# State space stage: real and imaginary parts of a group on the two halves of the partitions

## The chip, the cores and the metric

The kernel runs on one core of a Trainium2 chip. The metric is device time in microseconds for one call; the time before is the median of three runs. The core's engines are TensorE (PE, with its weight loads PEld), VectorE (DVE), ScalarE (ACT), GpSimd (POOL) and SyncE (SP), which issues transfers. Each takes its own instructions in a fixed order.

## The reference

The program is one step of a two-layer encoder: 2048 prompt positions and 8 samples of 16 positions, width 1024. Layer 0 is a diagonal complex state space mixer (S5), layer 1 a gated delta-rule mixer; each is normalised and modulated, and a last norm follows. The part that is changed is the core of layer 0. It has 64 groups of 16 channels, and each group has 64 complex states:

```python
def step(carry, uc):
    hr, hi = carry
    br = jnp.einsum('gpc,btgc->btgp', bbr, uc)
    bi = jnp.einsum('gpc,btgc->btgp', bbi, uc)
    pr, pi, sr, si = lax.associative_scan(_cplx_combine, (a_r, a_i, br, bi), axis=1)
    xr = pr * hr[:, None] - pi * hi[:, None] + sr
    xi = pr * hi[:, None] + pi * hr[:, None] + si
    y = jnp.einsum('gcp,btgp->btgc', c_re, xr) - jnp.einsum('gcp,btgp->btgc', c_im, xi)
    return (xr[:, -1], xi[:, -1]), y
```

In words: an input product gives a complex drive per state, a first-order complex recurrence runs over time, and an output product takes the real part of C times the state. The output then goes through a gelu, a gated linear unit and an output projection.

## The kernel before, in words

Time is cut into chunks of 8 positions, so a group's 16 channels times 8 positions fill 128 rows, and a chunk is one column: 256 columns of the prompt and 16 of the samples, 272 in all (`NCH`, with `NPC` = 256). Inside a chunk the recurrence is a small triangular matrix (`toe`) on the input; between chunks only the state matters.

The stage takes the 64 groups in 16 batches (`b`) of four: two pairs (`pl`), and in each pair two groups (`g2`, or `i`), one on partitions 0 to 63 and one on 64 to 127. So a state tile is `[128, 2 (pair), 2 (r: real, imaginary), 272]`: the partition halves are the two groups of a pair, and real and imaginary parts lie side by side in each partition.

`s5_setup(b)` makes a batch's matrices: VectorE builds the input matrix `abt` (L672 to L674), TensorE transposes it (L679) and ScalarE copies it out as `ab`; VectorE builds the output matrix `ca` (L685 to L687), which `split_w` splits into a high part (ScalarE's cast, L130) and a low part (VectorE's subtraction, L131) so that a product of three reduced-precision terms (high by high, high by low, low by high) keeps the precision; a product `pk` gives the triangular matrix, which is written to DRAM as `kp` (GpSimd clears it at L699, VectorE corrects it at L701, ScalarE issues the write at L702) and read back as `toe`.

`s5_main(b)` does the work. TensorE makes the drive `pb` for each pair (L732), ScalarE copies the sample columns out as `bs` (L735), VectorE turns by the rotation table into `f` (L737) and sums to `z` (L739, L740), scans two segments with a carry `cy` between them (L746 to L753), turns back into `t` (L760), and builds the states before each chunk, `x`, by a difference and a sum (L762, L763). The samples' columns of `x` come from the given states (L722) and L738. `x` is split into `xsh` and `xsl` like a weight (L130, L131). The output is one product `toe` by `u` (L772) and, per group, six products over its 64 partitions (L777): two parts by three terms. ScalarE applies the gelu (L781) and the result goes to DRAM.

TensorE has a second supply of work in the stage: the z projection, 64 blocks (`z_block`) of 24 products over 128 rows, called `pdz` in the trace, which depend on nothing in the stage. The last six blocks are held back behind the stage's last outputs. The weights of the next stage (`wgr`, split into `wg`) load into memory that the stage gives up at its end.

The order of each engine's instructions is fixed when the program is built: a scheduler plays the program through with its own durations and sets each engine's order by that. The buffers bound how far batches overlap: most tiles of `s5_main` have two buffers (pool `b2`), `kp` and the work tiles `tt` and `abt` one, `pb` one in PSUM, the outputs two.

Of the kernel before, what the change touches and what calls it, by code (L numbers as in the profile page):

```python
# [10 lines left out]
F32 = mybir.dt.float32  # L11
# [3 lines left out]
ALU = mybir.AluOpType  # L15
# [3 lines left out]
P = 128  # L19
# [3 lines left out]
NCH = 272  # L23
NPC = 256
# [29 lines left out]
def kernel(ctx: ExitStack, tc: tile.TileContext, I, O, upto="Z"):  # L54
# [19 lines left out]
    T, V, S, G, SY = (Engine(e) for e in (nc.tensor, nc.vector, nc.scalar, nc.gpsimd, nc.sync))  # L74
# [54 lines left out]
    def split_w(dst_hi, dst_lo, raw, lo_eng=None):  # L129
        S.copy(dst_hi, raw)  # L130
        (lo_eng or V).tensor_sub(dst_lo, raw, dst_hi.bitcast(F32))  # L131
# [102 lines left out]
    with ExitStack() as pa:  # L234
# [333 lines left out]
        for j in range(8):  # L568
            hh, hl = hcur
            T.ordered = j == 1  # L570
            for cb in range(8):
# [14 lines left out]
                if j > 0:  # L586
                    ps = psd4.tile([P, NCH], F32, tag="d", name=f"pd{j}_{cb}")
                    i_ = mm3(ps, ks(wu_hi[cb]), ks(wu_lo[cb]), hh, hl)
# [43 lines left out]
    with ExitStack() as pb:  # L632
        ps5 = pb.enter_context(ExitStack())
        b2 = ps5.enter_context(tc.tile_pool(reuse_waits="tile", name="b2", bufs=2))
        b1 = ps5.enter_context(tc.tile_pool(reuse_waits="tile", name="b1", bufs=1))
# [25 lines left out]
        def s5_setup(b):  # L661
# [8 lines left out]
            tt = b1.tile([P, 2, 2, 9, 16], F32, tag="tt", name=f"abtt{b}")  # L670
# [13 lines left out]
            for l in range(2):  # L684
                V.tensor_mul(ca[:, l], bc(bc(ccv[:, 0, l], 1, 9), 1, 2), bc(pw[:, l, 1:3], 3, 16))  # L685
                V.tensor_mul(t2[:, l], bc(bc(ccv[:, 1, l], 1, 9), 1, 2), bc(pw[:, l, 0:2], 3, 16))
            V.tensor_sub(ca, ca, t2)  # L687
            cs_ = [b2.tile([P, 2, 2, P], F32R, tag="ca" + i, name=f"ca{i}{b}") for i in "hl"]
            split_w(*(t.rearrange("p l r (n c) -> p (l r) n c", c=16) for t in cs_),
                    ca[:, :, :, 1:9].rearrange("p l r n c -> p (l r) n c"))  # L690
# [25 lines left out]
        def s5_main(b, u, tw, ca, ab, toe):  # L716
# [3 lines left out]
            xh = x[:, :, :, NPC:NCH].rearrange("p l r (q h) -> p l r q h", h=2)  # L720
            G.memset(x[:, :, :, 0:1], 0.0)
            S.copy(xh[:, :, :, :, 0], stN[:, prs])  # L722

# [4 lines left out]
            for pl in range(2):  # L728
# [9 lines left out]
                V.tensor_add(xh[:, pl, :, :, 1], ax[:, 2 * b + pl], bsv[:, :, :, 0])  # L738
            V.tensor_add(z[:, :, 0], f[:, 0, :, 0], f[:, 1, :, 1])  # L739
# [22 lines left out]
            V.tensor_sub(x[:, :, 0, 1:NPC], t[:, 0, :, 0, 0:m], t[:, 1, :, 1, 0:m])  # L762
            V.tensor_add(x[:, :, 1, 1:NPC], t[:, 0, :, 1, 0:m], t[:, 1, :, 0, 0:m])  # L763
# [4 lines left out]
            for pl in range(2):  # L768
# [4 lines left out]
                for r in range(2):  # L773
                    for wi, xi in ((0, 0), (0, 1), (1, 0)):
                        for i in range(2):
                            ln = slice(64 * i, 64 * i + 64)
                            i_ = T.matmul(pys[i], lhsT=ca[wi][ln, pl, r], rhs=xs[xi][ln, pl, r],  # L777
                                          start=False, stop=(r == 1 and wi == 1), tile_position=(64 * i, 0))
# [41 lines left out]
    with ExitStack() as px:  # L820
# [104 lines left out]
        for j in range(8):  # L925
# [78 lines left out]
            r = acc  # L1004
# [1094 lines left out]
```

## Time and profile before

| What | us |
|---|---|
| Median of 3 runs | 2154.48 |
| Lowest and highest | 2152.29, 2161.67 |
| Span of the profiled execution (it has no time listed beside this) | 2147.2 |
| TensorE busy | 2083.9 (97%) |
| VectorE busy | 1558.8 (73%) |
| ScalarE busy | 980.2 (46%) |
| GpSimd busy | 473.6 (22%) |

The page's shares are means over a long program; TensorE's 97% is modelled from pipelined matmuls, whose rows overlap: where the trace gives 0.29 us for one, the next starts 0.125 us later. The state space stage takes about 316 of the 2147 us. A row of the timeline gives the start, the duration of the group, engine, line, operation, written and read tile with partitions by elements, and a count; a form 64*128 is a matmul over 64 rows, and 128*128 one over 128.

### The profile page before, as it was taken

The page shows a single profiled execution, that of the slowest core. Times are in us where ns is not written, and L with a number is a line of the kernel's source. Part 1 is how long each engine was busy: PE and PEld are TensorE (multiplying, and loading weights), DVE is VectorE, ACT ScalarE, POOL GpSimd, SP SyncE. Part 2 cuts the span into 40 slices and gives each one's busy share as a digit, 9 for nine tenths or more (in the row PEclk, how much of TensorE's full clock was granted, in tenths as well). Part 3 has the DMA queues.
Part 4 walks back from the last instruction along what each step waited for, and adds up shares of the span by engine and source line. Part 5 has one row for each costly group of instructions (what it writes and reads, how often), then busy time and mean ns, then how long its engine had stood idle before and what let it go on. Part 6 is the DMA issues. An engine that isn't in the chain of part 4 may idle for free.

```text
span 2147.2 us, 42222 instructions
## 1 busy us (share of the span) xinstructions
PE 2083.9 (97%) x15729; PEld 1851.3 (86%) x15729; DVE 1558.8 (73%) x4017; ACT 980.2 (46%) x2298; POOL 473.6 (22%) x720
## 2 busy tenths in 40 slices
PE   6899999999799999999999999999999899999998
PEld 4888988888599999999888879889987688888887
DVE  6999498999756554446665669688556788888875
ACT  3543433333255544446665422341224556666663
POOL 1267310000112322222100000100011344444430
PEclk9999999999899999999999999999999999999999
DMA  9897744444386533336465313663456844444432
GB/s 278 273 299 234 239 150 149 141 157 148 97 242 220 190 113 110 108 100 218 138 202 171 92 50 86 162 146 103 135 169 217 269 143 126 134 142 147 147 113 70
DMA packets 398666, 344.99 MB, mean 161 GB/s; under 512 B 88410, under 2 KB 359274, under 8 KB 398460
## 3 DMA queue, kind: packets, MB, share of 16 engines
q1 hardware_dynamic: 261388, 234.95, 36.9%
q10 hardware_dynamic: 134256, 99.69, 14.4%
q0 software_dynamic: 2816, 7.65, 1.0%
q8 instruction: 124, 2.03, 0.4%
q14 instruction: 82, 0.67, 0.1%
HBM read 221.40 MB, written 120.80 MB: 159 GB/s over the span
## 4 chain that ended last, share of the span: by engine, by line
PE 86%; DVE 6%; DMA 4%; ACT 2%; issue 1%; SPq 1%; POOL 0%; ACTq 0%; DVEq 0%
PE epo L69 6%; PE pc L150 5%; PE pc L152 5%; PE pc L151 5%; PE pz L152 3%; PE po L150 3%; PE pz L151 3%; PE pdz L151 3%; PE pz L150 3%; PE po L152 3%; PE po L151 3%; PE pdz L150 3%; PE pdz L152 3%; PE pg L152 3%; PE pg L150 3%; PE pg L151 3%
## 5 line engine op out<-in xcount | busy, mean ns | idle before, releaser
L150 PE MATMUL pc<-h1h,wdh 128*128 128x512 f32 (+1 forms) x600 | 216.5, 361 | 0.0
L152 PE MATMUL pc<-h1h,wdl 128*128 128x384 f32 (+1 forms) x600 | 214.9, 358 | 0.0
L151 PE MATMUL pc<-h1l,wdh 128*128 128x384 f32 (+1 forms) x600 | 214.8, 358 | 0.1
L1414 DVE SCALAR_TENSOR_TENSOR ac<-pb,convw,ac 128x384 f32<-128x384 f32 (+3 forms) x288 | 163.6, 591 | 3.3
L150 PE MATMUL pdz<-hhz,wzh 128*128 128x272 f32 x512 | 152.3, 298 | 1.8 <-ACT evz L627 1.8
L151 PE MATMUL pdz<-hlz,wzh 128*128 128x272 f32 x512 | 153.0, 299 | 0.0
L152 PE MATMUL pdz<-hhz,wzl 128*128 128x272 f32 x512 | 151.6, 296 | 0.0
L150 PE MATMUL po<-gh,woh 128*128 128x272 f32 x512 | 148.6, 292 | 2.2 <-ACT gh L942 2.2
L151 PE MATMUL po<-gl,woh 128*128 128x272 f32 x512 | 148.4, 291 | 0.8 <-DVE gl L942 0.8
L152 PE MATMUL po<-gh,wol 128*128 128x272 f32 x512 | 148.7, 292 | 0.0
L151 PE MATMUL pg<-yl,wgh 128*128 128x272 f32 x512 | 148.4, 290 | 0.0
L150 PE MATMUL pg<-yh,wgh 128*128 128x272 f32 x512 | 147.5, 288 | 0.5 <-ACT evz L627 0.5
L152 PE MATMUL pg<-yh,wgl 128*128 128x272 f32 x512 | 147.5, 288 | 0.0
L150 PEld LDWEIGHTS pc<-h1h,wdh 128*128 128x128 f32 x600 | 112.6, 188 | 12.3 <-issue 1.7
L151 PEld LDWEIGHTS pc<-h1l,wdh 128*128 128x128 f32 x600 | 112.7, 188 | 10.4 <-issue 0.8
L152 PEld LDWEIGHTS pc<-h1h,wdl 128*128 128x128 f32 x600 | 112.6, 188 | 10.2 <-issue 0.8
L150 PE MATMUL pd<-hh,wuh 128*128 128x272 f32 x384 | 112.5, 294 | 0.0
L69 PE MATMUL epo<-w2h,ohi 128*128 128x512 f32 x272 | 111.7, 410 | 0.0
L152 PE MATMUL pd<-hh,wul 128*128 128x272 f32 x384 | 110.9, 289 | 0.0
L151 PE MATMUL pd<-hl,wuh 128*128 128x272 f32 x384 | 110.6, 288 | 0.0
L69 PE MATMUL epo<-w2l,ohi 128*128 128x512 f32 x272 | 107.5, 395 | 1.6 <-DMA w2l<-w2l_d 1.5
L939 POOL TENSOR_TENSOR zt<-zt,sz 128x272 f32<-128x272 f32 x64 | 63.4, 996 | 203.5 <-ACT sz L938 194.3
(613 smaller groups left out, 6373.7 us busy)
## 6 DMA issues: line engine op xcount, KB each, us to landing
wa<-in_w_ada SPq DMA_DIRECT2D x32, 512.0 KB
wdr<-in_w_in SPq DMA_DIRECT2D x24, 512.0 KB
h_d<-x ACTq DMA_DIRECT2D x8, 1088.0 KB
u_d<-ev ACTq DMA_DIRECT2D x64, 136.0 KB
hz<-h_d SPq DMA_DIRECT2D x16, 544.0 KB
u<-u_d SPq DMA_DIRECT2D x16, 544.0 KB
z_d<-evz ACTq DMA_DIRECT2D x64, 136.0 KB
y_d<-y ACTq DMA_DIRECT2D x32, 272.0 KB
```

Of the source, the lines that this page charges most:

```text
L69: i_ = f(*a, **kw)
L150: T.matmul(ps, lhsT=w_hi[k], rhs=x_hi[k], start=(k == 0), stop=False)
L151: T.matmul(ps, lhsT=w_hi[k], rhs=x_lo[k], start=False, stop=False)
L152: i_ = T.matmul(ps, lhsT=w_lo[k], rhs=x_hi[k], start=False, stop=(k == n - 1))
L939: G.tensor_mul(zt, zt, sz)
L1414: V.scalar_tensor_tensor(o, src(j), convw[:, b, j:j + 1], o, op0=ALU.mult, op1=ALU.add)
```

## The change

The output product is to contract over the real and the imaginary part of one group at once. For that `x` gets another layout: real parts on partitions 0 to 63 and imaginary parts on 64 to 127, with the group of the pair beside them in the free dimension, `[128 (r, state), 2 (pair), 2 (g2), 272]`. `ca` gets the same one. What stands before (`pb`, `f`, `z`, the scans, `t`) keeps the old layout.

So there are new steps. In `s5_setup` ScalarE copies four quarters of `ca` into a new tile `cax` (it shares the single buffer `tt`), and the split reads that. In `s5_main` the sample columns are built in a tile of their own, `xh`, and ScalarE copies four quarters of it into `x`. The difference and the sum that build `x` become four operations over 64 partitions each: two stay on VectorE (they move data to the other half), two go to GpSimd (they keep it in its half). Each group's output is then three products over 128 rows in place of six over 64.

```diff
             V.tensor_sub(ca, ca, t2)
+            cx = b1.tile([P, 2, 2, 9, 16], F32, tag="tt", name=f"cax{b}")
+            for r in range(2):
+                for g2 in range(2):
+                    S.copy(cx[64 * r:64 * r + 64, :, g2, 1:9], ca[64 * g2:64 * g2 + 64, :, r, 1:9])
             cs_ = [b2.tile([P, 2, 2, P], F32R, tag="ca" + i, name=f"ca{i}{b}") for i in "hl"]
-            split_w(*(t.rearrange("p l r (n c) -> p (l r) n c", c=16) for t in cs_),
-                    ca[:, :, :, 1:9].rearrange("p l r n c -> p (l r) n c"))
+            split_w(*(t.rearrange("p l g (n c) -> p (l g) n c", c=16) for t in cs_),
+                    cx[:, :, :, 1:9].rearrange("p l g n c -> p (l g) n c"))
...
-            xh = x[:, :, :, NPC:NCH].rearrange("p l r (q h) -> p l r q h", h=2)
+            xh = b2.tile([P, 2, 2, 8, 2], F32, tag="xh", name=f"xh{b}")
             G.memset(x[:, :, :, 0:1], 0.0)
             S.copy(xh[:, :, :, :, 0], stN[:, prs])
+            halves = (slice(0, 64), slice(64, 128))
...
+            for r, rl in enumerate(halves):
+                for g2, gl in enumerate(halves):
+                    S.copy(x[rl, :, g2, NPC:NCH], xh[gl, :, r].rearrange("p l q h -> p l (q h)"))
...
-            V.tensor_sub(x[:, :, 0, 1:NPC], t[:, 0, :, 0, 0:m], t[:, 1, :, 1, 0:m])
-            V.tensor_add(x[:, :, 1, 1:NPC], t[:, 0, :, 1, 0:m], t[:, 1, :, 0, 0:m])
+            for r, op in enumerate((ALU.subtract, ALU.add)):
+                for g2, gl in enumerate(halves):
+                    (G if g2 == r else V).tensor_tensor(x[halves[r], :, g2, 1:NPC], t[gl, 0, :, r, 0:m],
+                                                        t[gl, 1, :, 1 - r, 0:m], op=op)
...
-                for r in range(2):
-                    for wi, xi in ((0, 0), (0, 1), (1, 0)):
-                        for i in range(2):
-                            ln = slice(64 * i, 64 * i + 64)
-                            i_ = T.matmul(pys[i], lhsT=ca[wi][ln, pl, r], rhs=xs[xi][ln, pl, r],
-                                          start=False, stop=(r == 1 and wi == 1), tile_position=(64 * i, 0))
+                for wi, xi in ((0, 0), (0, 1), (1, 0)):
+                    for i in range(2):
+                        i_ = T.matmul(pys[i], lhsT=ca[wi][:, pl, i], rhs=xs[xi][:, pl, i], start=False, stop=(wi == 1))
```

Line numbers after the change are higher by up to 10 (the output products stand at L785, `t` at L768, `x` at L772).

The scheduler plays the new program through and moves instructions all over the stage. On TensorE, at the output products of batch 0's first pair (`py_0` and `py_1` are the two groups' outputs, `pdz` the z projection):

```order
+L785 MATMUL py_0_4277<-xsl_4273,cah_4147 128x272
+L785 MATMUL py_1_4278<-xsl_4273,cah_4147 128x272
+L785 MATMUL py_0_4277<-xsh_4272,cal_4148 128x272
+L785 MATMUL py_1_4278<-xsh_4272,cal_4148 128x272
 L150 MATMUL pdz_1_6555<-hhz_1_6355,wzh_4040 128x272
 L151 MATMUL pdz_1_6555<-hlz_1_6356,wzh_4040 128x272
 L152 MATMUL pdz_1_6555<-hhz_1_6355,wzl_4041 128x272
-L777 MATMUL py_0_4260<-xsl_4256,cah_4142 128x272
-L777 MATMUL py_1_4261<-xsl_4256,cah_4142 128x272
-L777 MATMUL py_0_4260<-xsh_4255,cal_4143 128x272
-L777 MATMUL py_1_4261<-xsh_4255,cal_4143 128x272
```

Before, six more rows of the other part follow; now four rows finish what ten did.

On TensorE again, where the z projections of the stage end. Before, they last until just ahead of the outputs of batch 14 (`py_0_6136`) and the drive of batch 15 (`pb_0_6180`):

```order
L150 MATMUL pdz_1_7971<-hhz_1_7771,wzh_4040 128x272
L151 MATMUL pdz_1_7971<-hlz_1_7772,wzh_4040 128x272
L152 MATMUL pdz_1_7971<-hhz_1_7771,wzl_4041 128x272
L772 MATMUL py_0_6136<-u_5907,toe_5948 128x272
L772 MATMUL py_1_6137<-u_5907,toe_5948 128x272
L732 MATMUL pb_0_6180<-u_6041,ab_6054 64x272 x4
L732 MATMUL pb_1_6189<-u_6041,ab_6054 64x272 x4
```

Now they end inside the outputs of batch 11 (`py_0_5751` to `py_3_5766`), ahead of the drive of batch 12 (`pb_1_5844`):

```order
L785 MATMUL py_1_5752<-xsh_5746,cal_5543 128x272
L151 MATMUL pdz_1_7971<-hlz_1_7772,wzh_4040 128x272
L152 MATMUL pdz_1_7971<-hhz_1_7771,wzl_4041 128x272
L737 MATMUL pb_1_5844<-u_5644,ab_5657 64x272 x4
L699 MATMUL pk_5814<-ca_5798,sp_5782 32x128 x4
L782 MATMUL py_2_5765<-u_5510,toe_5556 128x272
L785 MATMUL py_2_5765<-xsh_5746,cah_5542 128x272
```

The same z products thus lie in twelve batches instead of fourteen.

On GpSimd, about batches 2 to 4. Before there were only memsets (`kp` of batches 5 and 6, the first column of `x` of batches 3 to 5):

```order
L721 MEMSET xs_4614 128x4
L699 MEMSET kp_4737 64x112
L721 MEMSET xs_4748 128x4
L699 MEMSET kp_4871 64x112
L721 MEMSET xs_4882 128x4
```

Now the two operations on `x` of batches 2 and 3 (`xs_4490`, `xs_4624`) stand between them:

```order
L703 MEMSET kp_4613 64x112
L772 TENSOR_TENSOR xs_4490<-t_4532 64x2x255 x2
L725 MEMSET xs_4758 128x4
L703 MEMSET kp_4747 64x112
L772 TENSOR_TENSOR xs_4624<-t_4666 64x2x255 x2
```

So `x` of a batch now queues behind the clearing of `kp` for a batch two further on.

## The prediction

> **What bounds the kernel now.** I read the busy times by stretch first, then the waits, then the ends of the chain, and last the timelines of TensorE and VectorE inside the stage. By stretch (busy time of each engine, granted clock, DMA share):
>
> ```profile
> core 0: us, PE busy (x) PEld busy (x) DVE busy (x) ACT busy (x) POOL busy (x), PEclk, DMA share, GB/s
> 270.00:310.00 40.00, 40.00 (x322) 35.08 (x320) 39.07 (x81) 13.39 (x31) 5.69 (x13) 1.00 0.42 130
> 310.00:550.00 240.00, 240.00 (x1845) 199.77 (x1843) 219.12 (x467) 83.48 (x209) 3.54 (x24) 1.00 0.49 150
> 550.00:586.00 36.00, 25.31 (x148) 17.58 (x146) 30.63 (x54) 7.81 (x21) 8.43 (x9) 0.78 0.23 80
> ```
>
> The state space stage lasts from 270 to 586 us. In its middle TensorE never rests and VectorE works 219.12 of 240 us: two engines near their limit, the second with 9% to spare. At the end TensorE is short of work, and VectorE sets the pace. The waits inside the stage (in total, times, longest) and the end of the chain:
>
> ```profile
> DVE f L737 <- ACT bs L735: 20.4, 10, 4.5
> ACT bs L735 <- PE pb L732: 29.0, 23, 4.0
> ...
> 584.83 0.60 DVE xs L763
> 585.66 0.34 SPq L796
> 586.05 4.61 DMA wgr<-in_w_glu
> ```
>
> VectorE's spare time is 20.4 us of waiting at L737 for the input product pb, which comes late from TensorE's queue behind z projections. The chain shows what the stage's end decides: only when the last x is built do the next stage's weights start to load. So what the stage loses reaches the end of the kernel.
>
> Where x is complete gives the pace, batch 0 and batch 11:
>
> ```profile
> 301.84 0.68 DVE L763 TENSOR_TENSOR xs<-t 128x510 f32<-128x510 f32 x1
> 512.97 0.68 DVE L763 TENSOR_TENSOR xs<-t 128x510 f32<-128x510 f32 x1
> ```
>
> 211.1 us for 11 batches, 19.2 each; then 73.1 us to 586.
>
> **The output products.** TensorE's timeline around one group of them:
>
> ```profile
> 308.78 0.29 PE L151 MATMUL pdz<-hlz,wzh 128*128 128x272 f32 x1
> 308.91 0.28 PE L152 MATMUL pdz<-hhz,wzl 128*128 128x272 f32 x1
> 309.12 0.39 PE L777 MATMUL py<-xsl,cah 64*128 64x272 f32 x2
> 309.35 0.29 PE L777 MATMUL py<-xsh,cal 64*128 64x272 f32 x2
> 309.47 0.29 PE L777 MATMUL py<-xsh,cah 64*128 64x272 f32 x2
> 309.60 0.29 PE L777 MATMUL py<-xsl,cah 64*128 64x272 f32 x2
> 309.73 0.29 PE L777 MATMUL py<-xsh,cal 64*128 64x272 f32 x2
> 309.94 0.39 PE L150 MATMUL pdz<-hhz,wzh 128*128 128x272 f32 x1
> 310.18 0.29 PE L151 MATMUL pdz<-hlz,wzh 128*128 128x272 f32 x1
> ```
>
> A full product over 128 rows takes a slot of 0.125 us (308.78 to 308.91). A pair of the old products, one on each half of the rows, also takes one slot: the two run side by side. So 24 half products make 12 slots a batch, and the 12 full products of the change make 12 slots: halving their number saves nothing in itself. What goes is entering and leaving the half-row form: from 308.91 to 310.18 stand seven slots (0.88 us) in 1.27 us, 0.39 us too much per group. The order has 48 groups, three a batch: 1.17 us a batch, 18.7 us in all, are saved on TensorE.
>
> **What x costs now.** VectorE keeps two operations a batch, over 64 partitions instead of 128 and as long per partition (510 elements). I take the old 0.60 us from start to start for each: partitions don't set the time, elements do. Nothing is saved there. GpSimd gets two more, which VectorE did before. An operation of that length on GpSimd, and what it does to VectorE, stands in two places: a row of groups, and batches 14 and 15, the same VectorE work without and with GpSimd at work.
>
> ```profile
> L1219 POOL TENSOR_TENSOR olo<-ob,ohi 128x512 fp32r<-128x512 f32 x30 | 37.8, 1282 | 130.6 <-ACT ohi L69 130.6
> ```
>
> ```profile
> 559.47 0.69 DVE L739 TENSOR_TENSOR z<-f 128x512 f32<-128x512 f32 x1
> 560.08 0.68 DVE L740 TENSOR_TENSOR z<-f 128x512 f32<-128x512 f32 x1
> 560.68 1.36 DVE L746 TENSOR_TENSOR_SCAN z<-rN,z 128x128 f32<-128x128 f32 x4
> ...
> 562.55 0.86 DVE L746 TENSOR_TENSOR_SCAN z<-rN,cy,z 128x128 f32<-128x128 f32 x2
> ...
> 572.39 1.78 DVE L739 TENSOR_TENSOR z<-f 128x512 f32<-128x512 f32 x1
> 574.10 1.10 DVE L740 TENSOR_TENSOR z<-f 128x512 f32<-128x512 f32 x1
> 575.12 3.04 DVE L746 TENSOR_TENSOR_SCAN z<-rN,z 128x128 f32<-128x128 f32 x4
> ...
> 580.10 1.61 DVE L746 TENSOR_TENSOR_SCAN z<-rN,cy,z 128x128 f32<-128x128 f32 x4
> ```
>
> ```profile
> 571.41 2.20 POOL L797 TENSOR_TENSOR ax<-ax,bs 128x512 f32<-128x512 f32 x1 [18.89 <-DVE xs L738]
> 573.70 0.96 POOL L648 TENSOR_TENSOR stN<-ax,a 128x256 f32<-128x256 f32 x1
> ...
> 578.76 1.29 POOL L799 TENSOR_TENSOR stN<-stN,bs 128x512 f32<-128x512 f32 x1
> ```
>
> L739 takes 1.78 instead of 0.69 us while GpSimd's 512-element operation runs: 1.09 us lost. Over the whole stretch (559.47 to 562.55 against 572.39 to 580.10) VectorE loses 4.63 us to eight GpSimd operations of 2560 elements together, which is 0.92 us for 510. The upper bound is GpSimd's own 1.28 us. I take 1.1, the row of the nearest shape: 2.2 us a batch, 35 us over 16 batches (bounds 29 and 41). It falls on nearly every operation that follows in VectorE's order, since those too combine two tiles in SBUF; the lower end of all, nothing, is the first rival.
>
> The Trainium skill, SBUF — State Buffer, section Who interferes with whom, has a rule for this: a VectorE operation with two inputs in SBUF and a GpSimd operation that reads SBUF share a read interface, and the later waits for the whole of the other. By that rule each would cost the full 1.28 us and my sum would be some 6 us higher; the trace agrees in kind and lies a little below.
>
> **The other edits.** ScalarE gets eight copies a batch. Rows to price them:
>
> ```profile
> L130 ACT CAST xsh<-xs 128x1088 fp32r<-128x1088 f32 x16 | 17.6, 1100 | 16.9 <-DVE xs L763 14.7 <-DMA z_d<-evz 2.2
> L130 ACT CAST cah<-ca 128x512 fp32r<-128x512 f32 x16 | 9.9, 620 | 39.2 <-PE py L777 32.9 <-DMA k_d<-kp 3.6 <-DVE ca L687 2.8
> ```
>
> That is 0.83 ns an element, so 0.41 us for each of four copies of 256 elements into cax, and some 0.22 for each of four of 32 into x: 2.5 us a batch beside the 83.48 of 240 us that ScalarE works now, so it fits. The cax copies lie a batch ahead of their use, with VectorE work between ca and the low part; the copies into x wait for nothing late. If that cover failed, each batch would pay the 2.2 us of the copies and the cast. No DMA is added: SP has 579 rows before and now.
>
> What grows is the way from t to the low part of x: formerly two operations and the cast, 1.2 + 1.1 us; now two of GpSimd and two of VectorE in turns and the cast, some 3.8 + 1.1 us. Behind it on VectorE stands xsl, and behind that the next batch's f. In most batches three or four operations stand ahead of xsl and fill the cast's time as before; in batch 10 and three of the last four there is only the sum into xh (old L738), and about 1.2 us each is bare.
>
> **The sum, stretch by stretch.** *Batch 0:* VectorE is full (39.07 of 40), so its 2.2 us count: +2 (0 to 5).
>
> *Batches 1 to 11:* the new order puts 1132 z products there instead of 965 (counted from the last output product of batch 0 to that of batch 11). TensorE: 167 more slots are +20.9 us, 33 groups less are -12.9, so 219.1 instead of 211.1 us. VectorE: 219.12/240 of 19.2 is 17.5 us a batch, plus 2.2 is 19.7, or 216.7 us. Two engines that need 219 and 217 us and wait for each other at pb and at x don't both stay full. Before, the spare of VectorE (1.7 us a batch) let TensorE run without a gap; I allow 1 us a batch of new waiting: 230, +19. Bounds: +8 (no new waiting) and +28 (VectorE's 1.7 us of waiting stays, and GpSimd costs 1.28).
>
> *Batches 12 to 15:* no z product is left there in the new order (but for the last 20, inside batch 15's outputs), so VectorE decides. Its operations in the new order, each priced from start to start as in batch 14, are 47 us for f to xsl of four batches and 13 for the setup that is left; the old GpSimd work at the end takes 4.6, the new 8.8, the bare waits 3.6: 77 against 73.1, so +5 with the last batch's longer way (0 to 9). TensorE's clock falls there (0.78 already in the last 36 us), but each pb has ten or more us of VectorE work ahead of its use, or x and xsl; I add nothing.
>
> Together +26. The profiled execution would span 2173 instead of 2147.2 us; the median of the runs shown is 7.3 us above that span, so I add to the median: 2154.5 + 26 = 2180. The forecast's own range, by the three bounds, is 2162 to 2197.
>
> **The rivals.** *GpSimd doesn't hold VectorE up here, and the saved switches carry.* It speaks for it that VectorE waits 20.4 us anyway and that GpSimd is nearly idle (3.54 of 240); against it L739's 1.78 us. Then the middle goes by TensorE, +8, and the last batches by VectorE without the 8.8 us and without the earlier waits, 60 + 4.6 = 65 us against 73, -8: no change, 2154. It decides if an operation of GpSimd costs VectorE under about 0.3 us. Should also the 8 us of z products hide in ScalarE's and VectorE's waits of the middle, it is 2146.
>
> *GpSimd's queue delays x.* Memsets of kp now stand ahead of x in the same queue, and each waits for the DMA that reads the batch before:
>
> ```profile
> POOL kp L699 <- DMA k_d<-kp: 172.4, 15, 16.3
> ```
>
> So far nobody waited behind it. If it makes x 1.5 us late in each of 16 batches, 24 us come on top: 2204. Against it, in the order kp's correction on VectorE stands ten us or more before that x in all but one batch.
>
> **How the numbers follow.** Forecast 0.62, first rival 0.21 (a third of it below no change), second rival 0.13, something unseen 0.04. The time is the forecast's, 2180. The range goes from 2157, inside the first rival, to 2205, the second's time. A measurement here tells 0.5% from no change, that is 2143.7 to 2165.3: faster 0.07 (the third of the first rival), same 0.18 (its rest and the forecast's low edge), slower 0.75.
>
> **What would show it.** Right: no 64*128 form is left, and output products cost 0.125 us each with no gap around them; L672 to L690 and the scans on VectorE keep their length where GpSimd rests, while those behind t grow by about 1 us twice a batch; GpSimd's x operations last 1.3 to 2.2 us; TensorE idles over the last four batches; the first wgr load starts near 612 instead of 586. Wrong: VectorE's busy time in the stage grows by under 10 us (first rival), or GpSimd waits for k_d while VectorE waits for xsh (second); a pace of batches 1 to 11 under 19.9 or over 21.8 us would break the middle term.

## The result and the profile after

The changed kernel takes 2179.23 us (median of 4 runs, 2177.92 to 2180.46), the kernel before 2153.39 us beside it: ratio 1.0114, 95% interval 1.0095 to 1.0132. It is 25 us slower. The forecast was 2180.

Its profiled execution spans 2177.8 us. For one reading the reader has to know that the profiled execution of before (2147.2 us) was among the quickest of its kernel, whose medians in five comparisons were 2153 to 2158 us. Differences between profiles therefore come out some 5 us larger than the ratios. Below, prices come from ratios, and places from profiles.

Busy time by engine, first the whole program before, then after:

```profile
PE 2083.9 (97%) x15729; PEld 1851.3 (86%) x15729; DVE 1558.8 (73%) x4017; ACT 980.2 (46%) x2298; POOL 473.6 (22%) x720
```

```profile
PE 2076.7 (95%) x15537; PEld 1852.6 (85%) x15537; DVE 1582.1 (73%) x4017; ACT 1018.3 (47%) x2426; POOL 535.0 (25%) x752
```

VectorE executes as many instructions as before, two of the old ones a batch being half as wide now, and is busy 23.3 us longer. GpSimd has 32 instructions and 61 us more, ScalarE 128 and 38 us more. TensorE is 7.2 us less busy, and that is all the saved output products show.

The stretches of the stage after the change, without its first 40 us (busy time of PE, PEld, DVE, ACT and POOL, granted clock, DMA share and GB/s); the last of them belonged to the next stage before:

```profile
310.00:550.00 240.00, 230.36 (x1705) 202.91 (x1703) 220.57 (x422) 108.24 (x292) 37.41 (x43) 1.00 0.47 144
550.00:586.00 36.00, 20.97 (x82) 12.97 (x83) 34.73 (x70) 10.66 (x31) 6.88 (x8) 0.58 0.26 79
586.00:618.00 32.00, 12.17 (x53) 7.17 (x51) 27.43 (x45) 8.52 (x25) 13.64 (x12) 0.73 0.21 69
```

TensorE now rests 9.6 us in the middle, where it had none to spare. At the end it works about half of the time, and VectorE nearly all of it. The end of the stage, in the chain of waits:

```profile
610.87 2.37 DVE t L768 x2
...
613.26 0.69 DVE xs L772
613.96 1.65 DVE xs L772
615.64 1.15 DVE fsp L801
...
617.37 3.91 DMA wgr<-in_w_glu
```

The next stage's first weights start to load at 617.4 instead of 586.05 us, and from there to the end both kernels need the same (1560.4 and 1561.2 us). So the loss lies ahead of that point. Some of it was there when the stage began: VectorE's first operation on `abt` (L672) starts at 270.68 us in this profile and at 267.10 in the one of before, 3.6 us late.

The same, cut where VectorE starts the low part of x (`xsl`, L131) in batch 0, in batch 11 and in batch 15; before and after:

```profile
304.24:515.10 210.86, 210.86 (x1623) 175.34 (x1622) 194.47 (x412) 74.05 (x182) 3.25 (x22) 1.00 0.49 152
515.10:586.65 71.55, 60.21 (x418) 46.84 (x417) 60.90 (x119) 20.71 (x53) 8.83 (x12) 0.88 0.34 108
```

```profile
307.27:539.90 232.63, 225.71 (x1680) 200.58 (x1680) 215.04 (x410) 102.49 (x275) 37.41 (x43) 1.00 0.47 146
539.90:617.90 78.00, 40.44 (x179) 25.13 (x178) 70.32 (x130) 25.01 (x73) 20.63 (x21) 0.69 0.25 79
```

These 15 batches took 282.4 us and take 310.6. VectorE's busy time in them (third of the busy columns) was 255.4 and is 285.4; what is left is its waiting, 27.0 and 25.3. From x to x the stage is longer by VectorE's work, and its old waiting time has not shrunk to pay for that. Of the 30 us more work some 23 are new by the page; the rest is mostly preparation of matrices that lay ahead of batch 0's x before.

### The profile page after: what moved, and what is told of

The parts are those of the page before. It is cut to its first block, busy times and chain, and to the rows that moved or that the text cites. A ratio compares the mean times of both kernels' runs of the same rounds, so it can differ in the third digit from the quotient of the medians.

```text
span 2177.8 us, 41988 instructions
## 1 busy us (share of the span) xinstructions
PE 2076.7 (95%) x15537; PEld 1852.6 (85%) x15537; DVE 1582.1 (73%) x4017; ACT 1018.3 (47%) x2426; POOL 535.0 (25%) x752
## 4 chain that ended last, share of the span: by engine, by line
PE 71%; DVE 15%; DMA 7%; ACT 3%; issue 3%; POOL 1%; SPq 1%; ACTq 0%; DVEq 0%; POOLq 0%
PE epo L69 7%; PE pc L150 5%; PE pc L152 5%; PE pc L151 5%; PE pz L152 3%; PE pz L151 3%; PE pz L150 3%; PE po L150 3%; PE po L152 3%; PE po L151 3%; PE pg L152 2%; PE pg L150 2%; PE pg L151 2%; PE epx L69 2%; PE pdz L150 2%
## 5 line engine op out<-in xcount | busy, mean ns | idle before, releaser
L150 PE MATMUL pc<-h1h,wdh 128*128 128x512 f32 (+1 forms) x600 | 216.6, 361 | 0.2 <-ACT pb L1410 0.2
```

Source lines behind the costliest of these rows:

```text
L150: T.matmul(ps, lhsT=w_hi[k], rhs=x_hi[k], start=(k == 0), stop=False)
```

## The experiments

Each variant changes some lines, and with them the scheduler's order of the whole stage; its price is that of the edit and of the order that comes with it. The table sums up; "x to x" is the stretch from batch 0's `xsl` to batch 15's, with VectorE's busy time and its waiting in it. These three columns come from one profile of each kernel, and that of before was a quick one, so that differences of some 5 us to its row say little.

| Kernel | Ratio to before | x to x | VectorE busy | waiting |
|---|---|---|---|---|
| before | 1 | 282.4 | 255.4 | 27.0 |
| the change | 1.0114 | 310.6 | 285.4 | 25.3 |
| before + products over 128 rows | 1.0006 | 287.4 | 254.6 | 32.7 |
| before + x shared with GpSimd | 1.0061 | 292.9 | 282.4 | 10.5 |
| before + ScalarE's copies | 1.0030 | 294.1 | 259.1 | 35.0 |
| change, GpSimd clears instead | 1.0036 | 296.1 | 262.2 | 33.9 |
| change without the copies | 1.0039 | 295.0 | 282.0 | 13.0 |
| change, z projection spread | 1.0059 | 300.5 | 284.9 | 15.6 |
| change, all of x on VectorE | 1.0086 | 305.7 | 281.4 | 24.4 |
| before + ScalarE's copies, `cax` in its own buffer | 1.0025 | 282.6 | 251.8 | 30.8 |
| change, z projection spread, `cax` in its own buffer | 1.0071 | 294.6 | 272.6 | 22.0 |

### The output products alone

```diff
-                for r in range(2):
-                    for wi, xi in ((0, 0), (0, 1), (1, 0)):
-                        for i in range(2):
...
+                for wi, xi in ((0, 0), (0, 1), (1, 0)):
+                    for i in range(2):
+                        i_ = T.matmul(pys[i], lhsT=ca[wi][:, pl, i], rhs=xs[xi][:, pl, i], start=False, stop=(wi == 1))
```

> The kernel before, with only the output products made three over 128 rows in place of six over 64; x and ca keep the old layout, so the outputs of this stage are not the reference's. VectorE, ScalarE and GpSimd have the work of before. Theory: TensorE loses the 0.39 us of every entry into the half-row form, 18.7 us, but VectorE at 289 us of work in the stage is the next bound, so 2145 to 2153 us. Rival (the packing of the z products costs 25 us): the order has 1110 z products in batches 1 to 11 and only 26 in the last four, nearly as in the change, so 2172 to 2180.

Measured: 2155.88 us against 2155.18, ratio 1.0006 (0.9994 to 1.0018). The products alone are worth nothing, neither a gain nor a loss; neither the theory's gain nor the rival's loss came. This order packs the z projection nearly as the change does, so the packing together with TensorE's saving costs nothing; the run doesn't tell the two apart. The two stretches from x to x:

```profile
304.80:522.31 217.51, 216.42 (x1635) 193.68 (x1634) 195.00 (x413) 77.18 (x189) 3.27 (x22) 1.00 0.50 154
522.31:592.15 69.84, 42.90 (x230) 29.88 (x228) 59.63 (x117) 17.98 (x46) 7.93 (x12) 0.77 0.28 93
```

TensorE's saving shows (259.3 us busy from x to x instead of 271.1), but VectorE's work stands at 254.6 us as before and now waits 32.7. With less to do on TensorE the scheduler put the z projection earlier, TensorE stayed full in the middle and idle at the end. It had no use for the time, as far as the run shows.

### x shared with GpSimd, alone

```diff
-            V.tensor_sub(x[:, :, 0, 1:NPC], t[:, 0, :, 0, 0:m], t[:, 1, :, 1, 0:m])
-            V.tensor_add(x[:, :, 1, 1:NPC], t[:, 0, :, 1, 0:m], t[:, 1, :, 0, 0:m])
+            for r, op in enumerate((ALU.subtract, ALU.add)):
+                for g2, gl in enumerate((slice(0, 64), slice(64, 128))):
+                    (G if g2 == r else V).tensor_tensor(x[gl, :, r, 1:NPC], t[gl, 0, :, r, 0:m],
+                                                        t[gl, 1, :, 1 - r, 0:m], op=op)
```

> The kernel before, with only the building of x cut into four operations over 64 partitions, two of them on GpSimd as in the change, in the old layout; products, ca and sample columns as before. Theory: VectorE is held by 0.9 us for each of 32 operations, 30 us in the stage, and waits for TensorE as before: 2173 to 2182 us. Rival (order and packing): 992 z products in batches 1 to 11 against 965, 3 us of TensorE: 2154 to 2160.

Measured: 2166.66 us, ratio 1.0061 (1.0042 to 1.0080): +13 us, between the two. Its busy times in the whole program, and then its two stretches from x to x (PE, PEld, DVE, ACT, POOL):

```profile
PE 2087.9 (97%) x15729; PEld 1852.2 (86%) x15729; DVE 1588.6 (73%) x4017; ACT 979.9 (45%) x2298; POOL 532.8 (25%) x752
```

In the program VectorE is busy 29.8 us longer than before.

```profile
306.94:529.91 222.97, 217.48 (x1651) 180.92 (x1650) 217.66 (x420) 74.88 (x187) 38.19 (x44) 0.99 0.47 146
529.91:599.82 69.91, 57.68 (x381) 43.75 (x379) 64.70 (x112) 19.07 (x50) 21.32 (x20) 0.85 0.34 108
```

That is for 32 operations on GpSimd, 0.93 us each, so the holding is real. But the time grows by less than half of that, and VectorE's waiting falls from 27.0 to 10.5 us: the old waiting is a cushion that takes up half of the loss. In the change the cushion stays at 25 us; why, the next runs had to show.

### GpSimd's two operations as clears

```diff
-                    (G if g2 == r else V).tensor_tensor(x[halves[r], :, g2, 1:NPC], t[gl, 0, :, r, 0:m],
-                                                        t[gl, 1, :, 1 - r, 0:m], op=op)
+                    if g2 == r:
+                        G.memset(x[halves[r], :, g2, 1:NPC], 0.0)
+                    else:
+                        V.tensor_tensor(x[halves[r], :, g2, 1:NPC], t[gl, 0, :, r, 0:m], t[gl, 1, :, 1 - r, 0:m], op=op)
```

> The change, with GpSimd's two operations replaced by memsets of the same columns, which read nothing (half of x is zero, so the outputs of this stage are not the reference's). The order has the same 1132 z products in batches 1 to 11 and none in batches 12 to 14. Theory: with no reading by GpSimd VectorE isn't held, works 289 us in the stage, and the time is 2147 to 2157 us. Rival (order and packing): 2174 to 2180, as the change.

Measured: 2162.89 us, ratio 1.0036 (1.0023 to 1.0049). GpSimd keeps its instructions and their place in its order but reads nothing, and 0.78% of the change's 1.14% are gone, some 17 us. Its busy times in the whole program:

```profile
PE 2072.2 (96%) x15537; PEld 1850.8 (86%) x15537; DVE 1558.4 (72%) x4017; ACT 1019.4 (47%) x2426; POOL 491.2 (23%) x752
```

The group of its own operations on x (count, busy us, mean ns):

```profile
L775 DVE TENSOR_TENSOR xs<-t 64x510 f32<-64x510 f32 x32 | 21.9, 684 | 0.7
```

VectorE's work is back at 1558.4 us, and its own half of x takes 684 ns, as long as the operations over twice the partitions took before. That alone doesn't tell GpSimd's reading from its being at work, since a clear takes 0.52 us instead of 1.56, and without t to wait for it comes 7 us or more ahead of VectorE's x. But six pairs of the clears run beside a pair of operations of VectorE on `cat` (L686), which take both inputs from SBUF:

```profile
318.40 0.82 DVE L686 TENSOR_TENSOR cat<-sp 128x288 f32<-128x288 f32 x2
318.63 1.09 POOL L773 MEMSET xs<- 64x510 f32 x2
```

These two take 0.82 us, as they do without GpSimd (0.83 in the kernel before), and so do the other five pairs. So a clear at work doesn't hold VectorE there; GpSimd's operations that read t do. The kernel is still 8 us slower than before, which the theory did not foresee.

### All of x on VectorE

```diff
-                    (G if g2 == r else V).tensor_tensor(x[halves[r], :, g2, 1:NPC], t[gl, 0, :, r, 0:m],
+                    V.tensor_tensor(x[halves[r], :, g2, 1:NPC], t[gl, 0, :, r, 0:m],
                                                         t[gl, 1, :, 1 - r, 0:m], op=op)
```

> The change, with all four operations that build x on VectorE and none on GpSimd. Theory (GpSimd's two operations a batch hold VectorE up, 30 us in the stage by the two traces): VectorE gets two operations of 0.60 us a batch more (+19 us) and loses the 30 us of being held, so about 2168 us, 11 under the change; no operation behind t grows. Rival (the order with the z products packed into twelve batches costs the time): the order still has 1120 z products in batches 1 to 11 (1132 in the change), so 2178.

Measured: 2172.77 us, ratio 1.0086 (1.0054 to 1.0119), between the two and with an interval that overlaps the change's. Its busy times in the whole program:

```profile
PE 2078.6 (96%) x15537; PEld 1855.5 (85%) x15537; DVE 1582.3 (73%) x4049; ACT 1020.4 (47%) x2426; POOL 476.6 (22%) x720
```

Its group of operations on x, now four a batch:

```profile
L772 DVE TENSOR_TENSOR xs<-t 64x510 f32<-64x510 f32 x64 | 43.7, 683 | 0.7
```

VectorE is busy 1582.3 us, as in the change (1582.1). Doing the two operations itself costs VectorE as much work as GpSimd's doing them: handing them over had gained nothing.

### Two buffers for kp

```diff
-            kp = b2.tile([64, 240], F32, tag="kp", bufs=1, name=f"kp{b}")
+            kp = b2.tile([64, 240], F32, tag="kp", bufs=2, name=f"kp{b}")
```

> The change with two buffers for kp instead of one, so that the clearing of kp on GpSimd no longer waits for the DMA that reads the batch before, and nothing in GpSimd's queue can delay its operations on x. The order of TensorE's and the other engines' work stays as in the change. Theory (GpSimd's reading holds VectorE up, its queue doesn't matter): no difference to the change, 2177 to 2181 us. Rival (GpSimd's queue delays x): most of the queue's price comes back, 2155 to 2165 us.

Measured: 2181.99 us, ratio 1.0116 (1.0094 to 1.0138), the change's 1.0114 again. GpSimd's queue costs nothing that can be measured, and the second rival falls. In the change itself, by its waits (in total, times, longest), one cast of x waited for GpSimd, for 3.3 us; GpSimd's 76.8 us of waiting for kp's DMA do not show in the time:

```profile
ACT xsh L130 <- POOL xs L772: 3.3, 1, 3.3
POOL kp L703 <- DMA k_d<-kp: 76.8, 12, 12.7
```

### The z projection spread again

The change had packed the z projection into batches 0 to 11. Here each block from number 11 on (they count from 0) is held behind a batch's outputs, about as before.

```diff
+            outs.append(ends[1])
...
-            with later([ends[zst["n"] > 58]] if zst["n"] > 57 else []):
+            n = zst["n"]
+            with later([ends[n > 58]] if n > 57 else [outs[(n - 11) * 4 // 15]] if n > 10 else []):
```

> The change with the z projection spread again over batches 1 to 13 as evenly as before the change: each of the blocks 11 to 57 is held back behind the outputs of the batch 4(n-11)/15. Batches 1 to 11 then have 986 z products instead of 1132. Nothing else is changed. Theory (GpSimd's holding makes VectorE full, and the packed z products keep TensorE full at the same time, so that both wait for each other): TensorE's need in batches 1 to 11 falls by some 18 us, VectorE's waits of 19 us there shrink to about 10, the last four batches stay as long: 2168 to 2174 us. Rival (VectorE alone sets the pace, where the z products lie is all one): 2177 to 2181 us.

Measured: 2168.58 us, ratio 1.0059 (1.0040 to 1.0078). Half of the loss is gone by the order alone. Its two stretches from x to x:

```profile
305.30:533.38 228.08, 216.64 (x1576) 189.11 (x1574) 215.88 (x416) 100.65 (x270) 37.59 (x43) 0.99 0.47 145
533.38:605.81 72.43, 49.40 (x288) 38.02 (x287) 69.00 (x124) 27.34 (x78) 21.00 (x21) 0.83 0.30 95
```

VectorE works as long as in the change (284.9 us from x to x) and waits 15.6 instead of 25.3. That is the theory's sign: with both engines full, each wait of VectorE for TensorE counts; with TensorE at 216.6 of 228.1 us, the cushion pays. The last four batches became shorter as well (72.4 against 78.0), which the theory had not said.

The same spreading with GpSimd's clears:

> The change with both edits together: GpSimd's two operations on x are clears (half of x is then not the state, so the output is wrong), and the z blocks are spread over batches 1 to 13. With the clears alone 2162.9 us were measured, 8 us over the kernel before. Theory (those 8 us are the packing of the z products into batches 1 to 11, 1132 against 965): 2152 to 2158 us, about the kernel before. Rival (they are the longer way through the new copies and the two half operations on VectorE): 2161 to 2165 us.

Measured: 2162.05 us, ratio 1.0027 (1.0013 to 1.0041), against 1.0036 without the spreading; the intervals overlap. So the packing showed a cost only where VectorE was held. The 6 to 8 us that the clears left are something else, as the rival said.

### ScalarE's copies, alone and taken away

Alone: the kernel before with the eight copies a batch, in the old layout, so that nothing else changes.

```diff
+            cx = b1.tile([P, 2, 2, 9, 16], F32, tag="tt", name=f"cax{b}")
+            for r in range(2):
+                for g2 in range(2):
+                    S.copy(cx[64 * g2:64 * g2 + 64, :, r, 1:9], ca[64 * g2:64 * g2 + 64, :, r, 1:9])
...
+            for r in range(2):
+                for gl in (slice(0, 64), slice(64, 128)):
+                    S.copy(x[gl, :, r, NPC:NCH], xh[gl, :, r].rearrange("p l q h -> p l (q h)"))
```

> The kernel before with ScalarE's eight new copies a batch and nothing else: ca goes through four quarter copies (old layout) before its split, the sample columns of x are built in a tile of their own and come into x by four copies (old layout). x, the output products and GpSimd stay as before; the result is that of the kernel before. Theory of the prediction (the copies are hidden, ScalarE has room): 2153 to 2158 us, no difference. Rival (the copies delay what ScalarE hands to VectorE and TensorE, and are the 6 to 8 us that the change with GpSimd's clears still cost): 2160 to 2166 us.

Measured: 2164.56 us, ratio 1.0030 (1.0017 to 1.0043): +6.5 us for copies that were priced at nothing. Its two stretches:

```profile
304.12:522.04 217.92, 217.10 (x1637) 180.02 (x1634) 193.82 (x409) 99.34 (x266) 3.19 (x22) 1.00 0.49 149
522.04:598.18 76.14, 63.85 (x419) 47.63 (x414) 65.29 (x131) 28.59 (x82) 8.10 (x13) 0.86 0.31 100
```

ScalarE is busy 99 of 218 us, far from full, and yet VectorE waits 35.0 us instead of 27.0. The sum alone says little, since it was 32.7 with the products alone, at no cost in time. But its largest part, the waiting of f for `bs` (ScalarE's copy of the sample columns out of the drive `pb`), has changed its cause. An example from this run:

```profile
486.27 1.14 PE L736 MATMUL pb<-u,ab 128*64 128x272 f32 x8
487.32 0.41 ACT L691 COPY cax<-ca 64x256 f32<-64x256 f32 x1 [2.04 <-DVE ca L687]
...
489.31 0.40 ACT L691 COPY cax<-ca 64x256 f32<-64x256 f32 x1
489.74 0.18 ACT L739 COPY bs<-pb 128x32 f32<-128x32 f32 x1
489.95 1.29 DVE L741 TENSOR_TENSOR f<-pb,tw 128x512 f32<-128x512 f32 x2 [2.67 <-ACT bs L739]
```

pb is ready at 487.41, but ScalarE's queue has the four copies into `cax` ahead of `bs`, with two gelus between them (the rows left out), so that f starts 2.3 us later than pb would have let it. Of the 21.7 us of waiting at f from x to x, some 10 fall after pb was ready; in the kernel before it is 0.4 of 20.4, since there `bs` follows pb at once.

Taken away: the change without them.

```diff
-            cx = b1.tile([P, 2, 2, 9, 16], F32, tag="tt", name=f"cax{b}")
-            for r in range(2):
-                for g2 in range(2):
-                    S.copy(cx[64 * r:64 * r + 64, :, g2, 1:9], ca[64 * g2:64 * g2 + 64, :, r, 1:9])
...
-                    cx[:, :, :, 1:9].rearrange("p l g n c -> p (l g) n c"))
+                    ca[:, :, :, 1:9].rearrange("p l g n c -> p (l g) n c"))
...
-            xh = b2.tile([P, 2, 2, 8, 2], F32, tag="xh", name=f"xh{b}")
+            xh = x[:, :, :, NPC:NCH].rearrange("p l r (q h) -> p l r q h", h=2)
...
-            for r, rl in enumerate(halves):
-                for g2, gl in enumerate(halves):
-                    S.copy(x[rl, :, g2, NPC:NCH], xh[gl, :, r].rearrange("p l q h -> p l (q h)"))
```

> The change without ScalarE's eight copies: ca is split as it is and the sample columns are built straight in x, both in the old layout, so the output is wrong; GpSimd's and VectorE's operations on x and the products over 128 rows stay. Theory of the prediction (the copies are hidden): 2177 to 2181 us, as the change. Rival (the copies cost 6 to 8 us): 2169 to 2175 us.

Measured: 2165.22 us, ratio 1.0039 (1.0024 to 1.0054): 0.75% of the 1.14% gone, more than the rival had asked for. Its two stretches:

```profile
306.78:533.27 226.49, 217.09 (x1607) 190.62 (x1607) 219.10 (x421) 76.14 (x189) 35.12 (x44) 1.00 0.48 149
533.27:601.75 68.48, 42.36 (x243) 31.40 (x241) 62.91 (x110) 17.93 (x46) 20.93 (x20) 0.78 0.29 93
```

GpSimd holds VectorE as in the change (282.0 us busy from x to x), but the waiting is down to 13.0 us. This is the cushion that the change lacked: without the copies it takes up the holding as it did in the kernel before (10.5 with x shared alone), with them it does not.

### Whose time the copies take

The tile `cax` shares its single buffer with work tiles of VectorE. Does VectorE wait for that buffer, or is it ScalarE's own time? With a buffer for `cax` alone:

```diff
-            axt = b1.tile([P, 32, 8], F32, tag="abtt", name="axt")
+            axt = b2.tile([P, 32, 8], F32, tag="z", name="axt")
...
-            cx = b1.tile([P, 2, 2, 9, 16], F32, tag="tt", name=f"cax{b}")
+            cx = b1.tile([P, 2, 2, 9, 16], F32, tag="cax", name=f"cax{b}")
```

On the kernel with the copies alone:

> The kernel before with ScalarE's eight copies a batch, as in the run with the copies alone (2164.6 us, ratio 1.0030), but cax has a buffer of its own instead of sharing the single buffer tt with VectorE's work tiles (room for it comes from the scratch tile of the state advance, which now shares z's buffers). So VectorE's next abtt and cat no longer wait until the copies have been cast and split. Theory A (the shared buffer makes the copies' price): 2154 to 2159 us, ratio under 1.0015. Theory B (ScalarE's own time does, by making it late for bs, xsh and evz): 2162 to 2167 us.

Measured: 2163.43 us, ratio 1.0025 (1.0011 to 1.0038), no different from 1.0030. And on the change with the z projection spread:

> The change with the z blocks spread over batches 1 to 13 (measured: 2168.6 us, ratio 1.0059) and, in addition, cax in a buffer of its own. The result is the reference's. Theory A (the shared buffer makes the copies' price): some 6 us less, 2159 to 2164 us. Theory B (ScalarE's own time does): 2166 to 2172 us. By both it stays slower than the kernel before, since GpSimd's reading still adds some 27 us to VectorE's work.

Measured: 2173.22 us, ratio 1.0071 (1.0053 to 1.0089) against 1.0059. By the ratios the buffer is not the cost, neither alone nor in the change. The profiles don't bear that out so simply. With its own buffer `cax` no longer makes `bs` late (0.4 of 15.8 us of waiting at f fall after pb was ready), and the copies alone take 282.6 us from x to x, as the kernel before (282.4); but that stretch starts 9.9 us later than in the run with the shared buffer (313.99 against 304.12), of which 4.8 were there at the stage's first `abt` (273.27 against 268.47). The other pair is alike: 294.6 against 300.5 us, from 313.01 on against 305.30. So with the shared buffer a part of the copies' price at least is `bs` standing behind them. What keeps the time up with a buffer of its own stays open: one profile of each doesn't tell whether its late start comes from the edit.

### A version meant to be better

VectorE makes the difference and the sum over all 128 partitions, ScalarE carries the four quarters over, GpSimd does nothing, and the z projection is spread.

```diff
+            V.tensor_sub(t[:, 0, :, 0, 0:m], t[:, 0, :, 0, 0:m], t[:, 1, :, 1, 0:m])
+            V.tensor_add(t[:, 0, :, 1, 0:m], t[:, 0, :, 1, 0:m], t[:, 1, :, 0, 0:m])
...
-                    (G if g2 == r else V).tensor_tensor(x[halves[r], :, g2, 1:NPC], t[gl, 0, :, r, 0:m],
-                                                        t[gl, 1, :, 1 - r, 0:m], op=op)
+                    S.copy(x[rl, :, g2, 1:NPC], t[gl, 0, :, r, 0:m])
```

> A version meant to be better: VectorE makes the difference and the sum over all 128 partitions as before (in place in t), ScalarE copies the four quarters into the new layout of x (about 0.6 us each, 2.4 us a batch), GpSimd has nothing to do with x, the output products go over 128 rows, and the z blocks are spread over batches 1 to 13. Theory (the cost is GpSimd's holding plus the packing of z): VectorE is back at some 289 us in the stage, and only the longer way from t to the low part of x is left, bare in a few batches: 2153 to 2160 us, no better than the kernel before by more than 0.1%, since VectorE sets the pace and the saved half-row switches are on TensorE. Rival (the new layout itself costs, by ScalarE's copies): 2165 to 2175 us.

Measured: 2177.46 us, ratio 1.0091 (1.0069 to 1.0113), worse than expected by some 20 us, and above the rival's range too. Its middle, and the group of its new copies:

```profile
310.42:540.88 230.46, 214.61 (x1541) 187.03 (x1539) 196.54 (x414) 128.78 (x314) 2.98 (x21) 0.96 0.46 144
```

```profile
L774 ACT COPY xs<-t 64x510 f32<-64x510 f32 x64 | 39.4, 616 | 9.6 <-DVE t L770 8.5 <-ACT evz L627 0.4
```

VectorE has no more work than before (196.5 us, against 194.5) and ScalarE is busy 129 of 230 us, yet the middle takes 20 us more. The four copies stand one behind the other between t and the cast, 2.5 us a batch, on the way from t to the split of x. That explains a part at most: of VectorE's 45.7 us of waiting from x to x, 6.3 are for the cast, and more is at kp (12.9) and f (8.5), whose reason here was not looked for further. None of the versions beats the kernel before.

## Why the prediction was right, and where it was not

**The sum held, its parts less.** 25 us slower came for 26 forecast. By stretch, from x to x: batch 0 +3.0 (307.27 against 304.24; forecast +2), batches 1 to 11 +21.8 (forecast +19), batches 12 to 15 +6.4 (forecast +5). The pace of the middle was 21.1 us a batch, inside the 19.9 to 21.8 that were set. The +3.0 is no sign for batch 0's term: 3.6 us were there at the stage's first `abt`. The first load of wgr, forecast near 612 us, came at 617.4. That the total agreed to a microsecond is in part luck, as the following terms show.

**The output products.** Right in that halving their number saves nothing; of the 18.7 us priced for the half-row form, TensorE's busy time shows 7.2 by the page in the change and 11.8 with the products alone (modelled ends), and alone they moved the time by nothing. After the change a group looks like this:

```profile
399.18 1.08 PE L782 MATMUL py<-u,toe 128*128 128x272 f32 x4
399.89 0.62 PE L785 MATMUL py<-xsh,cah 128*128 128x272 f32 x2
400.34 0.41 PE L785 MATMUL py<-xsl,cah 128*128 128x272 f32 x2
400.60 0.41 PE L785 MATMUL py<-xsh,cal 128*128 128x272 f32 x2
400.85 0.29 PE L151 MATMUL pdz<-hlz,wzh 128*128 128x272 f32 x1
```

No 64*128 form is left; the last four products cost 0.13 us each (400.34 to 400.85), the first pair behind the `toe` products 0.45, so not quite "no gap".

**What GpSimd's operations cost VectorE.** The step that failed, in the overlap: "35 us over 16 batches (bounds 29 and 41)", 1.1 us for each of 32 operations. Measured were 23.3 us in the change, 0.73 each, and 29.8 us alone, 0.93 each; the first is below the lower bound. The reason given there, that it falls on nearly every operation that follows "since those too combine two tiles in SBUF", overlooked f. Groups of the stage, before and then after the change:

```profile
L737 DVE TENSOR_TENSOR f<-pb,tw 128x512 f32<-128x512 f32 x64 | 41.3, 682 | 20.4 <-ACT bs L735 20.4
L763 DVE TENSOR_TENSOR xs<-t 128x510 f32<-128x510 f32 x16 | 10.9, 680 | 0.0
L672 DVE TENSOR_TENSOR abt<-sp 128x256 f32<-128x256 f32 x30 | 11.5, 414 | 0.5 <-PE abT L679 0.5
```

```profile
L742 DVE TENSOR_TENSOR f<-pb,tw 128x512 f32<-128x512 f32 x64 | 41.0, 683 | 8.9 <-ACT bs L740 8.9
L772 DVE TENSOR_TENSOR xs<-t 64x510 f32<-64x510 f32 x32 | 39.5, 1234 | 0.6
L672 DVE TENSOR_TENSOR abt<-sp 128x256 f32<-128x256 f32 x32 | 16.3, 547 | 0.4 <-PE abT L679 0.4
L772 POOL TENSOR_TENSOR xs<-t 64x510 f32<-64x510 f32 x32 | 50.1, 1564 | 112.3 <-DVE t L768 111.1
```

x on VectorE went from 680 to 1234 ns, 17.7 us in all, and L672 from 414 to 547, 4 us; but f, which reads pb from PSUM, takes 683 as before (682). The mean of 1234 mixes two kinds: 14 of the 32 took 0.68 to 0.69 us and 18 took 1.63 to 1.68. How this looks in the order of time, around batch 6's x (columns: start, duration, engine, line):

```profile
428.36 1.27 DVE L742 TENSOR_TENSOR f<-pb,tw 128x512 f32<-128x512 f32 x2
428.52 2.72 POOL L772 TENSOR_TENSOR xs<-t 64x510 f32<-64x510 f32 x2 [6.51 <-DVE t L768]
429.56 1.97 DVE L672 TENSOR_TENSOR abt<-sp 128x256 f32<-128x256 f32 x2
431.54 1.38 DVE L772 TENSOR_TENSOR xs<-t 64x510 f32<-64x510 f32 x2
```

GpSimd starts at 428.52 beside f, and f runs on at full speed to 429.63; two of L672, with both inputs in SBUF, take 1.97 us instead of 0.83 (2 x 414 ns). GpSimd is done at 431.24, and VectorE's x runs at full speed. Taken one by one, 24 operations of VectorE start beside one of GpSimd's and are lengthened, by 1.0 us on average and 24 us together, the 18 of x among them. Each of those 18 ends 0.54 to 0.55 us after the operation of GpSimd that it met, whenever it had started: it waits for that one's end. Eight of GpSimd's 32 lengthen nothing by more than 0.2 us; beside them VectorE runs f. So 1.1 us was near for each meeting, but not each of the 32 met. The Trainium skill, SBUF — State Buffer, section Who interferes with whom, says just this: a VectorE operation with at most one input in SBUF, outside its two-port modes, does not contend with GpSimd, and one with two inputs in SBUF contends with a GpSimd operation that reads SBUF, not with one that only writes it. Here f kept its 683 ns, and `cat` its 0.82 us a pair beside the clears, so the trace agrees. The whole 1.28 us for each of the 32, as the prediction applied the rule, was too high: 0.73 and 0.93 were measured, in the change because eight met no such operation and the others were already under way when VectorE's came.

**ScalarE's copies.** The step that failed by kind: "2.5 us a batch ... so it fits". They cost 6.5 us alone, and taking them from the change gave back 16. Room on an engine was taken for cover, but a copy also delays what stands behind it in ScalarE's queue: in the run with the copies alone `bs`, and with it f, came up to 2.3 us late behind `cax`, and in the change 5.8 of the 8.9 us of waiting at f fall after pb was ready, against 1.2 of 3.4 without the copies. So the forecast came out by two errors of opposite sign: GpSimd's term 12 us too large in VectorE's work, the copies' term missing.

**The new waiting.** "I allow 1 us a batch of new waiting" was 11 us, and put down to TensorE and VectorE both near full. That coupling is real: spreading the z projection gave back 12 us (1.0114 to 1.0059), and only while VectorE was held. But the copies were the other half of it: without them the cushion worked in the scheduler's own order, packed as it was (13.0 us of waiting). In the prediction's terms, of VectorE's 1.7 us of waiting a batch nearly all stayed (25.3 of 27.0 us from x to x).

**TensorE's clock.** Granted 0.58 and 0.73 at the end of the stage, lower than before (0.78); nothing was added for it, and the last four batches came out 1.4 us over the forecast. No run shows whether the clock has a part in that.

**The rivals.** GpSimd does hold VectorE (with x shared alone, with clears in its place, and operation by operation in the trace), so the first falls; its half about the switches falls with the products alone at 1.0006. The queue falls with two buffers for kp.

## What to carry to other kernels

An operation moved to GpSimd isn't free for VectorE: where both read two tiles in SBUF at the same time, VectorE paid here about what it would have cost to keep the operation, so first look at what VectorE runs then (f, with one input in PSUM, paid nothing). An engine that is less than half busy can still cost time with instructions added to its queue, as `cax` ahead of `bs` did here; price what stands behind them, not the engine's share. And look for the waits of the second busiest engine: they are a cushion for extra work, until something else, here the order of the filling work and a longer queue, uses them up.

## What the runs showed that was not expected

- Eight short copies a batch, 2.5 us on an engine that was busy 83.5 of 240 us, cost 6.5 us over 16 batches alone and 16 us where VectorE was held up too.
- A half-wide operation over 64 partitions takes as long as one over 128 (684 and 680 ns for 510 elements a partition).
- GpSimd's operation on x took from 1.25 to 2.26 us, 1.56 on average, against the 1.28 us, for 512 elements over 128 partitions, that the prediction took. The trace shows that GpSimd is held as well: beside f alone it took 1.25 to 1.29, and 2.26 where VectorE's `hlz` (two inputs in SBUF, 1.28 us) had started 0.16 us before it.
- Spreading the z projection over the batches was worth 12 us while VectorE was held up by GpSimd, and nothing measurable when it was not (1.0036 to 1.0027).
